# One transformer layer on one core: parts of 8, 6, 8 hidden units, x updates and one weight sum by adding transfers, interleaved down units, modulation sums dealt anew

## The chip, the cores and the metric

The kernel runs on one core of one Trainium2 chip. A core has a matrix engine (PE, with its weight loads listed as PEld), three elementwise engines (DVE, ACT, POOL) and a sync engine (SP) that mostly starts transfers; 16 DMA engines move the data. Each engine works through its own list of instructions in order and waits on semaphores for the others. The metric is the device time of one execution in microseconds: the median of the kernel before is 997.49 us over three runs (995.41 to 998.38). One more execution was profiled.

## The reference

One layer, sequence 512, width 1024, 16 heads of 64, hidden width 2816, all in float32:

```
mod = silu(c) @ w_mod + b_mod                # nine vectors of 1024: shift, scale, gate for each of three sub-layers
h = rms_norm(x, g_ffn1) * (1 + sc1) + sh1
x = x + 0.5 * (1 + ga1) * ((silu(h @ w1_gate) * (h @ w1_up)) @ w1_down)
h = rms_norm(x, g_mix) * (1 + sc2) + sh2
x = x + (1 + ga2) * mixer(h)                 # stick-breaking heads and forgetting heads, one projection in, one out
h = rms_norm(x, g_ffn2) * (1 + sc3) + sh3
x = x + 0.5 * (1 + ga3) * ((silu(h @ w2_gate) * (h @ w2_up)) @ w2_down)
```

The change touches the two feed-forward sub-layers (FFN1 and FFN2), the nine modulation vectors, and the first matmuls of the mixer.

## The kernel before, in words

**Layout and precision.** Activations lie transposed: x is eight tiles of 128 features by 512 positions. A product of two float32 matrices is made of three matmuls: each operand is split into a rounded "hi" and the rest "lo", and hi·hi, hi·lo and lo·hi are added up in PSUM (`mm3`, L129 to L132). `prep` (L122) makes a weight ready: SP starts the transfer into a `raw` tile, ACT casts it to `hi` (L125), DVE subtracts to get `lo` (L126). `raw`, `hi` and `lo` have four buffers each, so weights run ahead of their use by up to four tiles.

**A feed-forward sub-layer** (`ffn`) goes through 2816 = 22 x 128 hidden units in three parts, `FPARTS = (8, 8, 6)`. For each hidden unit of a part it makes gate and up, then `gated` (L406): ACT's silu, a DVE product `av`, ACT's cast `ah` (L414), DVE's rest `al` (L415). Then `down` multiplies the part's units by their rows of the down weight, for each of eight chunks e of 128 output features: 3 x 8 matmuls of 512 columns for a part of 8, 3 x 6 for a part of 6, into a PSUM bank of the tag `pt`, of which there are two. DVE then adds the scaled bank to x[e] (`update`, L574). So x is updated three times in each sub-layer.

**Pairs.** Units from number 8 on (FFN1) or 4 on (FFN2) are made two at a time by `block_pair` (L442): gate and up of both are a 2x2 block product done with 7 instead of 8 products, each 24 matmuls of 256 columns. It loads four weight blocks r11, r12, r21, r22 and makes s1 = r21+r22, s2 = s1-r11, s3 = r11-r21, s4 = r12-s2 by one DVE operation each (L459), each product's operand again cast by ACT (L453) and reduced to `lo` by DVE (L454). The products run in the order r11, s2, s1, r12, s3, s4, r22 and collect in three banks, `o`, `mm` and `z`.

**Modulation sums.** 56 of the 72 pieces of the modulation vectors are computed in the midst of FFN1, by `mod_next(n)`: SP loads a 512 KB tile `wm` and DVE does a multiply-and-sum (L216). `wm` has four buffers, which the DVE combinations s1 to s4 share. `mod_next` is called with 2 after units 4 to 7, with 1 after each pair, with 2 after each chunk e of a down, until none are left.

**The turn.** At the end of FFN1 and of the mixer, `turn` (L642) does the last three chunks (e5 to e7) in two halves of the sequence, H0 and H1, 256 columns each. While H1 of e5 to e7 runs, the mean square of H0 is taken (a matmul at L659, placed ahead of step 5 of e5's H1), then the inverse root, then the normalised `h` for H0 by DVE, ACT and DVE again. The first matmuls of the next stage, the V projection of the mixer (L724), begin as soon as h of H0 is there. They run for two groups of four banks; each bank is copied out when its eight k are done.

**Order.** PE's order is the order of the code. On the other engines a scheduler decides, by its own estimates; each engine's list is then fixed.

Of the kernel before, what the change touches and what calls it, by code (L numbers as in the profile page):

```python
# [8 lines left out]
F32 = mybir.dt.float32  # L9
# [6 lines left out]
P = 128  # L16
# [1 line left out]
D = 1024  # L18
KD = D // P
NF = 22  # L20
FPARTS = (8, 8, 6)
SPLIT1 = tuple(range(8, NF, 2))
SPLIT2 = tuple(range(4, NF, 2))
NPAIR = 4
# [11 lines left out]
def hybrid_layer(  # L36
# [74 lines left out]
    def bank(tag):  # L111
        return psum.tile([P, S], F32, tag=tag, name=nm(tag), bufs=PB[tag])
# [327 lines left out]
        return out  # L440

    def block_pair(w, n_w, j, T, tmp):  # L442
        raws = []
        for n in range(4):
            raw = wpool.tile([P, 2 * S], F32, tag="raw", name=nm("raw"), bufs=4)
            nc.sync.dma_start(raw, w[n_w + n])
            raws.append(raw)
        r11, r12, r21, r22 = raws

        def parts(src):  # L450
            hi = wpool.tile([P, 2 * S], F32R, tag="hi", name=nm("hi"), bufs=4)
            lo = wpool.tile([P, 2 * S], F32R, tag="lo", name=nm("lo"), bufs=4)
            nc.scalar.copy(hi, src)  # L453
            nc.vector.tensor_tensor(lo, src, hi.bitcast(F32), op=ALU.subtract)  # L454
            return hi, lo

        def combined(x0, x1, op):
            t = block_tile(tmp)
            nc.vector.tensor_tensor(t, x0, x1, op=op)  # L459
            return t  # L460

        def whole_h(k0, sl):
            return [(h["h"][k0 + k][:, sl], h["l"][k0 + k][:, sl]) for k in range(KD // 2)]

        def summed_h(n):
            sl = slice(n * 256, (n + 1) * 256)
            return [(hi[:, sl], lo[:, sl]) for hi, lo in T]

        def product(b, wt, rhs, first, last):
            for u, sl in enumerate((H0, H1)):  # L470
                for k, (rh, rl) in enumerate(rhs):
                    lh, ll = wk(wt, 4 * u + k)
                    f, e = first and u == 0 and k == 0, last and k == KD // 2 - 1
                    nc.tensor.matmul(b[:, sl], lh, rh, start=f, stop=False, skip_group_check=True)  # L474
                    nc.tensor.matmul(b[:, sl], lh, rl, start=False, stop=False, skip_group_check=True)  # L475
                    nc.tensor.matmul(b[:, sl], ll, rh, start=False, stop=e, skip_group_check=True)  # L476

        def result(x0, x1, out=None):
            if out is None:
                out = tmp.tile([P, S], F32, tag="bres", name=nm("bres"), bufs=4)  # L480
            nc.vector.tensor_tensor(out, x0, x1, op=ALU.add)
            return out

        bx, by, bz = bank("o"), bank("mm"), bank("z")
        product(bx, parts(r11), whole_h(0, H0), True, True)
        p1 = tmp.tile([P, S], F32, tag="bres", name=nm("bres"), bufs=4)
        nc.scalar.copy(p1, bx)
        s1 = combined(r21, r22, ALU.add)
        s2 = combined(s1, r11, ALU.subtract)
        product(by, parts(s2), summed_h(1), True, True)  # L490
        q = result(by, p1)
        product(bz, parts(s1), summed_h(0), True, True)
        r = result(bz, p1)
        product(bx, parts(r12), whole_h(4, H0), False, True)
        s3 = combined(r11, r21, ALU.subtract)
        product(by, parts(s3), summed_h(2), False, True)
        c22 = result(by, r, r)
        s4 = combined(r12, s2, ALU.subtract)
        product(bz, parts(s4), whole_h(4, H1), False, True)
        c12 = result(bz, q, q)  # L500
        product(by, parts(r22), summed_h(3), False, True)
        c21 = result(by, p1, p1)
        return [
            gated(j, [(H0, bx[:, H0], bx[:, H1]), (H1, c12[:, H0], c12[:, H1])], tmp),
            gated(j + 1, [(H1, c22[:, H0], c22[:, H1]), (H0, c21[:, H0], c21[:, H1])], tmp),
        ]

    def ffn(first, w, wd, gm, startup, boundary, tmp, finish=None, split=()):
        pend = list(kb) if startup else []
        blocks = {}  # L510
        n_w = 0
        f0 = 0
        for part, nf in enumerate(FPARTS):
            last_part = part == len(FPARTS) - 1
            a = []
            halves_first = first and part == 0
            units = {}
            j = -1
            while j + 1 < nf:
                j += 1  # L520
                f = f0 + j
                if f in split:
                    if "T" not in blocks:
                        blocks["T"] = block_sums(tmp)
                    a += block_pair(w, n_w, j, blocks["T"], tmp)
                    n_w += 4
                    j += 1
                    if startup:
                        mod_next(1)
                    continue  # L530
                ps = []
                for u in range(2):
                    if pend:
                        ps.append(pend.pop(0))
                        continue
                    if halves_first and j < 2:
                        if j == 0 and u == 0:
                            ws, bs = [], []
                            for i in range(4):
                                ws.append(prep(w[n_w], D, nc.gpsimd if i == 3 else None))  # L540
                                n_w += 1
                                bs.append(bank("mm" if i % 2 == 0 else "z"))
                            late = [(i, k) for i in range(4) for k in range(KD // 2, KD)]
                            for sl in (H0, H1):
                                early = [(i, k) for k in range(KD // 2) for i in range(4)]
                                for i, k in early + (late if sl is H1 else sorted(late, key=lambda s: s[1])):
                                    lh, ll = wk(ws[i], k)
                                    mm3(bs[i][:, sl], lh, ll, h["h"][k][:, sl], h["l"][k][:, sl], k == 0, k == KD - 1)
                                    if sl is H0 and (i, k) == (3, 0):
                                        finish()  # L550
                            in_order.__exit__(None, None, None)
                            units = dict(enumerate(bs))
                        ps.append(units[2 * j + u])
                        continue
                    wt = prep(w[n_w], D)
                    n_w += 1
                    b = bank("z" if u else "mm")
                    for k in range(KD):
                        lh, ll = wk(wt, k)
                        mm3(b, lh, ll, h["h"][k], h["l"][k], k == 0, k == KD - 1)  # L560
                    ps.append(b)
                a.append(gated(j, [(FULL, ps[0], ps[1])], tmp))
                if startup and f > 3:
                    mod_next(2 if part == 0 else 3)
            if startup and part == 0:
                blocks["T"] = block_sums(tmp)
            if last_part and boundary != "end":
                in_order.__enter__()
            done = down(wd, a, f0, nf, gm, boundary if last_part else None, tmp)
            f0 += nf  # L570
        return done

    def update(e, ps, gm, sl):
        nc.vector.scalar_tensor_tensor(  # L574
            out=x[e][:, sl], in0=ps[:, sl], scalar=g_col(gm)[:, e : e + 1], in1=x[e][:, sl], op0=ALU.mult, op1=ALU.add
        )

    def down(wd, a, f0, nf, gm, boundary, tmp):
        nfull = KD if boundary is None else KD - 1 if boundary == "end" else KD - NB
# [9 lines left out]
        def chunk(e):  # L589
            return wd[e, :, f0 * P : (f0 + nf) * P]  # L590

        for e in range(nfull):
            wt = prep(chunk(e), nf * P)
            ps = bank("pt")
            for step in steps(wt, ps, FULL):
                step()
            update(e, ps, gm, FULL)
            mod_next(2)
            if acc:
                acc.add(e)  # L600
            if boundary == "end":
                nc.scalar.dma_start(out[e], x[e])
# [141 lines left out]

    chunks = [v_weights(2), v_weights(3)]
    for sp in range(2):
        grp = [(ch, s, bank("mm" if s % 2 == 0 else "z")) for ch in chunks for s in (2 * sp, 2 * sp + 1)]
        for k in range(KD):
            for ch, s, b in grp:
                v_step(ch, s, k, b)  # L750
            if sp == 0 and k == 0:
                finish()
        for ch, s, b in grp:
            v_out(ch[0], s, b)
# [483 lines left out]
```

## Time and profile before

| | |
|---|---|
| median of 3 runs | 997.49 us |
| profiled execution | 999.74 us, of which the span 998.0 us |
| granted TensorE clock, mean over the span | 0.993 |
| PE busy | 976.3 us (98%), 6284 matmuls |
| DVE busy | 773.7 us (78%) |
| ACT busy | 439.0 us (44%) |
| POOL busy | 119.0 us (12%) |
| moved by DMA | 129.04 MB, mean 129 GB/s |

PE is busy nearly always, but "busy" is taken from modelled ends of matmuls that overlap, and a matmul that runs at half the clock counts as busy for twice as long. What a stage costs is read from the starts of its first and last matmul. A matmul of 512 columns that follows another without waiting starts 0.227 us after it (192 of them in the 43.52 us from 104.72 to 148.24), one of 256 columns 0.120 us after it. The stages of FFN1 lie as follows, in microseconds of the span: down of the first part 104.72 to 148.24, three pairs, the fourth, down of the second part 228.96 to 273.55, three pairs, down of the third part from 334.02, its halved chunks until 374.37, then the V projection. FFN2 ends the program; its last down begins at 961.13.

### The profile page before, as it was taken

Reading aid. Unit: us, or ns where it says so; the run is one execution under the profiler, and the core shown is the slowest. Engines: PE = TensorE matmul, PEld = TensorE weight load, DVE = VectorE, ACT = ScalarE, POOL = GpSimd, SP = SyncE. Lnnn points to the kernel's source line nnn. Section 1 sums busy time; section 2 is a strip of 40 time slices with the busy share of each in tenths; the row PEclk is TensorE's granted clock in tenths of the full one; section 3 lists DMA queues with packets and bytes.
Section 4 is the critical chain, followed back from the end, with each engine's and each line's share of the span. In section 5 each row is a group of like instructions: output and inputs, shape, how many; then the busy total and the mean of one; then the engine's idle time right before and its main releaser. Section 6 shows DMA issues by size and latency. Waiting matters only on the chain.

```text
span 998.0 us, 15752 instructions
## 1 busy us (share of the span) xinstructions
PE 976.3 (98%) x6284; PEld 869.4 (87%) x6284; DVE 773.7 (78%) x1147; ACT 439.0 (44%) x686; POOL 119.0 (12%) x131
## 2 busy tenths in 40 slices
PE   8999999999999898999999999999999999999998
PEld 7888889998899798877887877998988999889997
DVE  7999967999879966688857687698855699556962
ACT  6344224443244425587556462364432444324430
POOL 1000000000000043065413335210000000000000
PEclk9999999999999899999999999999999999999999
DMA  9985933359634832411212111214252133521231
GB/s 358 316 277 154 343 135 106 121 159 309 235 104 122 260 107 65 127 55 53 64 54 73 44 43 65 85 37 133 76 147 93 55 116 103 150 85 64 96 117 63
DMA packets 37369, 129.04 MB, mean 129 GB/s; under 512 B 4400, under 2 KB 4656, under 8 KB 37296
## 3 DMA queue, kind: packets, MB, share of 16 engines
q1 hardware_dynamic: 35712, 125.88, 38.1%
q10 hardware_dynamic: 1584, 2.16, 0.6%
q8 instruction: 49, 0.80, 0.3%
q14 instruction: 24, 0.20, 0.1%
HBM read 125.92 MB, written 2.10 MB: 128 GB/s over the span
## 4 chain that ended last, share of the span: by engine, by line
PE 76%; DVE 14%; ACT 4%; DMA 3%; issue 2%; POOL 1%; SPq 0%; ACTq 0%; DVEq 0%; POOLq 0%
PE pt L131 8%; PE pt L132 8%; PE pt L130 8%; PE mm L130 5%; PE mm L132 4%; PE mm L131 4%; PE mm L476 3%; PE mm L475 3%; PE mm L474 3%; PE o L476 3%; PE o L475 3%; PE o L474 2%; PE z L476 2%; PE z L475 2%; PE z L474 2%; DVE lo L454 2%
## 5 line engine op out<-in xcount | busy, mean ns | idle before, releaser
L125 ACT CAST hi<-raw 128x1024 fp32r<-128x1024 f32 (+2 forms) x90 | 91.5, 1021 | 142.3 <-PE pt L131 61.3
L131 PE MATMUL pt<-al,hi 128*128 128x512 f32 (+1 forms) x334 | 131.1, 392 | 2.5 <-DVE al L415 2.5
L130 PE MATMUL pt<-ah,hi 128*128 128x512 f32 (+1 forms) x334 | 130.4, 391 | 0.6 <-ACT ah L414 0.6
L132 PE MATMUL pt<-ah,lo 128*128 128x512 f32 (+1 forms) x334 | 130.4, 390 | 0.0
L126 DVE TENSOR_TENSOR lo<-raw,hi 128x1024 fp32r<-128x1024 f32 (+2 forms) x89 | 108.0, 1216 | 28.8 <-ACT hi L125 28.3
L453 ACT CAST hi<-bsum 128x1024 fp32r<-128x1024 f32 x64 | 66.8, 1051 | 113.5 <-DVE bsum L459 61.3
L474 PE MATMUL mm<-th,hi 128*128 128x256 f32 x384 | 108.7, 283 | 0.0
L475 PE MATMUL mm<-tl,hi 128*128 128x256 f32 x384 | 108.7, 283 | 0.0
L476 PE MATMUL mm<-th,lo 128*128 128x256 f32 x384 | 108.7, 283 | 0.0
L574 DVE SCALAR_TENSOR_TENSOR x<-pt,gcol,x 128x512 f32<-128x512 f32 (+1 forms) x51 | 36.3, 712 | 67.2 <-PE pt L132 67.2
L454 DVE TENSOR_TENSOR lo<-bsum,hi 128x1024 fp32r<-128x1024 f32 x64 | 78.2, 1222 | 10.8 <-ACT hi L453 10.3
L453 ACT CAST hi<-raw 128x1024 fp32r<-128x1024 f32 x48 | 50.4, 1050 | 67.5 <-PE pt L131 30.5
L130 PE MATMUL mm<-hh,hi 128*128 128x512 f32 (+1 forms) x208 | 79.6, 383 | 0.0
L132 PE MATMUL mm<-hh,lo 128*128 128x512 f32 (+1 forms) x208 | 77.9, 374 | 0.6 <-DVE lo L126 0.6
L131 PEld LDWEIGHTS pt<-al,hi 128*128 128x128 f32 x334 | 63.4, 190 | 16.8 <-DVE al L415 4.0
L131 PE MATMUL mm<-hl,hi 128*128 128x512 f32 (+1 forms) x208 | 77.8, 374 | 0.2 <-DVE hl L170 0.2
L130 PEld LDWEIGHTS pt<-ah,hi 128*128 128x128 f32 x334 | 63.3, 190 | 14.4 <-ACT ah L414 1.4
L132 PEld LDWEIGHTS pt<-ah,lo 128*128 128x128 f32 x334 | 63.4, 190 | 12.9
L474 PEld LDWEIGHTS mm<-th,hi 128*128 128x128 f32 x384 | 73.7, 192 | 0.0
L475 PEld LDWEIGHTS mm<-tl,hi 128*128 128x128 f32 x384 | 73.7, 192 | 0.0
L476 PEld LDWEIGHTS mm<-th,lo 128*128 128x128 f32 x384 | 73.7, 192 | 0.0
L476 PE MATMUL o<-hh,lo 128*128 128x256 f32 x256 | 72.4, 283 | 0.0
(349 smaller groups left out, 2565.6 us busy)
## 6 DMA issues: line engine op xcount, KB each, us to landing
raw<-w SPq DMA_DIRECT2D x80, 512.0 KB, 3.6
wm<-wmod SPq DMA_DIRECT2D x72, 512.0 KB, 5.2
raw<-w1d SPq DMA_DIRECT2D x16, 512.0 KB, 6.3
raw<-wqk SPq DMA_DIRECT2D x16, 512.0 KB, 3.5
raw<-w2d SPq DMA_DIRECT2D x16, 512.0 KB, 4.2
raw<-w1s SPq DMA_DIRECT2D x8, 512.0 KB, 5.3
raw<-wo SPq DMA_DIRECT2D x8, 512.0 KB, 3.5
raw<-w1d SPq DMA_DIRECT2D x8, 384.0 KB, 5.9
```

The costliest lines, as they stand in the source:

```text
L125: nc.scalar.copy(hi, raw)
L126: (lo_engine or nc.vector).tensor_tensor(lo, raw, hi.bitcast(F32), op=ALU.subtract)
L130: nc.tensor.matmul(ps, lh, rh, start=first, stop=False)
L131: nc.tensor.matmul(ps, lh, rl, start=False, stop=False)
L132: nc.tensor.matmul(ps, ll, rh, start=False, stop=last)
L453: nc.scalar.copy(hi, src)
L454: nc.vector.tensor_tensor(lo, src, hi.bitcast(F32), op=ALU.subtract)
L474: nc.tensor.matmul(b[:, sl], lh, rh, start=f, stop=False, skip_group_check=True)
L475: nc.tensor.matmul(b[:, sl], lh, rl, start=False, stop=False, skip_group_check=True)
L476: nc.tensor.matmul(b[:, sl], ll, rh, start=False, stop=e, skip_group_check=True)
L574: nc.vector.scalar_tensor_tensor(out=x[e][:, sl], in0=ps[:, sl], scalar=g_col(gm)[:, e : e + 1], in1=x[e][:, sl], op0=ALU.mult, op1=ALU.add)
```

## The change

Five things change:

1. `FPARTS` is (8, 6, 8) in both sub-layers: the second part has three pairs and the third four (FFN1).
2. In the first two parts of each sub-layer, x is no longer updated by DVE. ACT reads the bank and writes the scaled result to an SBUF tile (`add_far`, tag `bres`, four buffers), and a transfer started by POOL adds that tile to x[e]. 32 of the 51 updates move. The updates of the last part stay on DVE.
3. In `block_pair`, s1 = r21+r22 is made by transfers: SP loads r21 into the tile, and a transfer started by POOL adds r22 to it. r22 is also loaded by itself, so a pair has five transfers of 512 KB. s3 becomes r22-s2. The products run in the order r11, s1, s2, r12, s3, s4, r22.
4. In each down, the steps of e0 and e1 are interleaved: all but the last two units of e0, all but the last two units of e1, the last two of e0, the last two of e1.
5. `mod_next` is called with 4 after units 4 to 7, with 2 after a pair (1 for the pairs at 14 and 16 and 18, none at 20), and 2 after each e as before: the 56 sums end ahead of the third part's down. In the V projection, the second group uses the banks pt, mm, pt, o in place of mm, z, mm, z.

The halved chunks of the third part now have 8 steps of 3 matmuls in place of 6, and its five whole chunks 8 in place of 6.

```diff
-FPARTS = (8, 8, 6)
+FPARTS = (8, 6, 8)
...
     def block_pair(w, n_w, j, T, tmp):
-        raws = []
-        for n in range(4):
+        d11, d12, d21, d22 = (w[n_w + n] for n in range(4))
+
+        def load(src):
             raw = wpool.tile([P, 2 * S], F32, tag="raw", name=nm("raw"), bufs=4)
-            nc.sync.dma_start(raw, w[n_w + n])
-            raws.append(raw)
-        r11, r12, r21, r22 = raws
+            nc.sync.dma_start(raw, src)
+            return raw
+
+        s1 = load(d21)
+        nc.gpsimd.dma_start(s1, d22, accum_op=ALU.add)
+        r11, r12, r22 = load(d11), load(d12), load(d22)
...
-        s1 = combined(r21, r22, ALU.add)
+        product(bz, parts(s1), summed_h(0), True, True)
+        r = result(bz, p1)
         s2 = combined(s1, r11, ALU.subtract)
         product(by, parts(s2), summed_h(1), True, True)
         q = result(by, p1)
-        product(bz, parts(s1), summed_h(0), True, True)
-        r = result(bz, p1)
         product(bx, parts(r12), whole_h(4, H0), False, True)
-        s3 = combined(r11, r21, ALU.subtract)
+        s3 = combined(r22, s2, ALU.subtract)
...
-                        mod_next(1)
+                        mod_next(2 if f < 14 else 1 if f < NF - 2 else 0)
...
-                    mod_next(2 if part == 0 else 3)
+                    mod_next(4)
...
+    def add_far(e, ps, gm, tmp):
+        t = tmp.tile([P, S], F32, tag="bres", name=nm("step"), bufs=4)
+        nc.scalar.activation(t, ps, AF.Identity, scale=g_col(gm)[:, e : e + 1])
+        nc.gpsimd.dma_start(x[e], t, accum_op=ALU.add)
+
     def down(wd, a, f0, nf, gm, boundary, tmp):
...
-        for e in range(nfull):
+        ahead = {}
+        for e in range(2):
             wt = prep(chunk(e), nf * P)
             ps = bank("pt")
-            for step in steps(wt, ps, FULL):
+            ahead[e] = (ps, steps(wt, ps, FULL))
+            for step in ahead[e][1][: nf - 2]:
                 step()
-            update(e, ps, gm, FULL)
+        for e in range(nfull):
+            if e in ahead:
+                ps, left = ahead[e][0], ahead[e][1][nf - 2 :]
+            else:
+                wt = prep(chunk(e), nf * P)
+                ps = bank("pt")
+                left = steps(wt, ps, FULL)
+            for step in left:
+                step()
+            if boundary is None:
+                add_far(e, ps, gm, tmp)
+            else:
+                update(e, ps, gm, FULL)
             mod_next(2)
...
-        grp = [(ch, s, bank("mm" if s % 2 == 0 else "z")) for ch in chunks for s in (2 * sp, 2 * sp + 1)]
+        tags = iter(("pt", "mm", "pt", "o") if sp else ("mm", "z", "mm", "z"))
+        grp = [(ch, s, bank(next(tags))) for ch in chunks for s in (2 * sp, 2 * sp + 1)]
```

How this stands on three engines, in FFN1. Names carry the number of the instruction; `raw`, `hi` and `lo` are a weight and its two halves, `av`, `ah`, `al` a hidden unit and its two halves, `bw` the weights of the halved chunks, `wm` a modulation tile, `junk` the throw-away output of a modulation sum.

ACT, in the down of the first part, before:

```order
L414 CAST ah_847<-av_844 128x512
L125 CAST hi_1068<-raw_1067 128x1024
L105 ACTIVATE sg_921<-mm_865 128x512
L125 CAST hi_1108<-raw_1107 128x1024
L414 CAST ah_925<-av_922 128x512
L125 CAST hi_1149<-raw_1148 128x1024
L125 CAST hi_1189<-raw_1188 128x1024
L125 CAST hi_1229<-raw_1228 128x1024
L125 CAST hi_1269<-raw_1268 128x1024
```

and after the change:

```order
L414 CAST ah_951<-av_948 128x512
L437 CAST th_1016<-bsum_1009 128x1024
L125 CAST hi_1191<-raw_1190 128x1024
L583 ACTIVATE step_1076<-pt_1026,gcol 128x512
L125 CAST hi_1233<-raw_1232 128x1024
L583 ACTIVATE step_1093<-pt_1051,gcol 128x512
L125 CAST hi_1275<-raw_1274 128x1024
L583 ACTIVATE step_1135<-pt_1110,gcol 128x512
L583 ACTIVATE step_1177<-pt_1152,gcol 128x512
L125 CAST hi_1317<-raw_1316 128x1024
L583 ACTIVATE step_1221<-pt_1196,gcol 128x512
L583 ACTIVATE step_1263<-pt_1238,gcol 128x512
```

Between the casts now stand the activations that empty the banks, in the order e0, e1, e2 and so on. The one of e0 (`step_1076`) has the cast of e4's weight (`hi_1191`) ahead of it, that of e2 (`step_1135`) the cast of e6's.

DVE, from the end of the last pair into the third part's down, before:

```order
L126 TENSOR_TENSOR lo_3409<-raw_3407,hi_3408 128x768
L216 SCALAR_TENSOR_TENSOR junk_3435,mods<-wm_3433,c_bc 128x1024
L411 TENSOR_TENSOR av_3346<-sg_3345,bres_3194 128x256
L481 TENSOR_TENSOR bres_3160<-mm_3130,bres_3160 128x512
L216 SCALAR_TENSOR_TENSOR junk_3439,mods<-wm_3437,c_bc 128x1024
L415 TENSOR_TENSOR al_3352<-av_3346,ah_3351 128x512
L411 TENSOR_TENSOR av_3356<-sg_3355,bres_3160 128x256
L126 TENSOR_TENSOR lo_3447<-raw_3445,hi_3446 128x768
L216 SCALAR_TENSOR_TENSOR junk_3473,mods<-wm_3471,c_bc 128x1024
L415 TENSOR_TENSOR al_3362<-av_3356,ah_3361 128x512
L216 SCALAR_TENSOR_TENSOR junk_3477,mods<-wm_3475,c_bc 128x1024
L574 SCALAR_TENSOR_TENSOR x_80<-pt_3375,gcol,x_80 128x512
```

and after:

```order
L411 TENSOR_TENSOR av_3367<-sg_3366,bres_3245 128x256
L485 TENSOR_TENSOR bres_3183<-mm_3153,bres_3183 128x512
L415 TENSOR_TENSOR al_3373<-av_3367,ah_3372 128x512
L126 TENSOR_TENSOR lo_3494<-raw_3492,hi_3493 128x1024
L411 TENSOR_TENSOR av_3377<-sg_3376,bres_3183 128x256
L126 TENSOR_TENSOR bw_3566<-raw_3564,bw_3565 128x1024
L415 TENSOR_TENSOR al_3383<-av_3377,ah_3382 128x512
L126 TENSOR_TENSOR bw_3572<-raw_3570,bw_3571 128x1024
L126 TENSOR_TENSOR bw_3578<-raw_3576,bw_3577 128x1024
L577 SCALAR_TENSOR_TENSOR x_80<-pt_3392,gcol,x_80 128x512
L126 TENSOR_TENSOR lo_3530<-raw_3528,hi_3529 128x1024
L577 SCALAR_TENSOR_TENSOR x_81<-pt_3417,gcol,x_81 128x512
```

The modulation sums are gone from among the last two units' operations. In their place the subtractions for the halved chunks (`bw`) stand there, two of them between the last `al` and the update of x[0].

SP, at the start of the third part's down weights, before:

```order
L124 DMA raw_3369<-w1d 128x768
L124 DMA raw_3407<-w1d 128x768
L209 DMA wm_3365<-wmod 128x1024
L209 DMA wm_3395<-wmod 128x1024
L209 DMA wm_3401<-wmod 128x1024
L209 DMA wm_3433<-wmod 128x1024
L209 DMA wm_3437<-wmod 128x1024
L124 DMA raw_3445<-w1d 128x768
```

and after:

```order
L447 DMA raw_3150<-w 128x1024
L124 DMA raw_3386<-w1d 128x1024
L124 DMA raw_3411<-w1d 128x1024
L124 DMA raw_3456<-w1d 128x1024
L124 DMA raw_3492<-w1d 128x1024
L124 DMA raw_3528<-w1d 128x1024
L124 DMA raw_3564<-w1d 128x1024
L124 DMA raw_3570<-w1d 128x1024
```

The five modulation loads between the second and the third down weight are gone.

## The prediction

> **What bounds the kernel now.** I read first the page's busy times and the chain of waits that ended last, then the matmul engine's waits by releaser.
>
> ```profile
> PE 976.3 (98%) x6284; PEld 869.4 (87%) x6284; DVE 773.7 (78%) x1147; ACT 439.0 (44%) x686; POOL 119.0 (12%) x131
> PE 76%; DVE 14%; ACT 4%; DMA 3%; issue 2%; POOL 1%; SPq 0%; ACTq 0%; DVEq 0%; POOLq 0%
> PE mm L724 <- ACT hh L167: 2.8, 1, 2.8
> PE pt L131 <- DVE al L415: 2.5, 3, 1.1
> PE z L724 <- ACT V L713: 0.9, 1, 0.9
> PE pt L130 <- ACT ah L414: 0.6, 1, 0.6
> ```
>
> PE is the bound, with only 22 us (998.0 - 976.3) not busy. So taking work off DVE is worth nothing by itself; the change can win only where PE waits, or runs slowly after waiting. The four waits that it touches add up to 6.8 us, but what a wait costs is read from stages (start, length and PE's busy time; then clock, DMA share, GB/s):
>
> ```profile
> 104.72:148.24 43.52, 43.52 (x193) 1.00 0.63 233
> 228.96:273.55 44.59, 44.00 (x194) 1.00 0.76 274
> 334.02:360.58 26.56, 23.99 (x92) 0.87 0.63 211
> 374.37:381.86 7.49, 4.64 (x21) 0.77 0.48 142
> 961.13:990.03 28.90, 28.90 (x129) 1.00 0.23 82
> ```
>
> The first row is the first down of FFN1 and runs without loss: 192 matmuls of 512 columns, 43.52/192 = 0.2267 us each. The second is the same work and takes 1.07 us more. The third is FFN1's last down, 90 such matmuls, which should take 20.40 us and take 26.56: 6.16 lost. The fourth is the start of the V projection, the fifth the last down of FFN2 (126 matmuls, 28.57; 0.33 lost).
>
> **The last down of FFN1.** PE by time, the first steps of e0 and the slow stretch after them:
>
> ```profile
> 336.77 0.39 PE L130 MATMUL pt<-ah,hi 128*128 128x512 f32 x1
> 338.01 0.50 PE L131 MATMUL pt<-al,hi 128*128 128x512 f32 x1 [0.85 <-DVE al L415]
> 338.34 0.40 PE L132 MATMUL pt<-ah,lo 128*128 128x512 f32 x1
> 339.38 0.50 PE L130 MATMUL pt<-ah,hi 128*128 128x512 f32 x1 [0.64 <-ACT ah L414]
> 340.96 0.79 PE L131 MATMUL pt<-al,hi 128*128 128x512 f32 x1 [1.08 <-DVE al L415]
> 341.55 0.63 PE L132 MATMUL pt<-ah,lo 128*128 128x512 f32 x1
> 341.98 0.63 PE L130 MATMUL pt<-ah,hi 128*128 128x512 f32 x1
> 346.67 0.46 PE L132 MATMUL pt<-ah,lo 128*128 128x512 f32 x1
> ```
>
> e0 reaches units 4 and 5 at 336.8, 2.7 us after its start, before ah and al exist. It waits three times, and then 12 matmuls run 0.43 us apart (341.55 to 346.67): half rate, 2.4 us. The Trainium skill, "TensorE: Matmul & The Clock Gate", Part 1, says that an idle stretch halves the matmul clock until some 3.4 us of work have passed. By that rule the slow stretch goes with the waits; the trace agrees, with the granted clock of 0.87 in this stage.
>
> What made ah and al late, on ACT, DVE and SP:
>
> ```profile
> 317.78 9.59 SPq L209 DMA_DIRECT2D wm<-wmod  x5
> 327.41 0.42 SPq L124 DMA_DIRECT2D raw<-w1d  x1
> 333.99 0.83 ACT L125 CAST hi<-raw 128x768 fp32r<-128x768 f32 x1 [3.58 <-DMA raw<-w1d]
> 336.12 1.22 DVE L216 SCALAR_TENSOR_TENSOR junk<-wm,c_bc 128x1024 f32<-128x1024 f32 x1
> 336.68 1.28 ACT L98 ACT_TABLE_LOAD   x1
> 338.72 0.61 ACT L414 CAST ah<-av 128x512 fp32r<-128x512 f32 x1
> 339.07 1.22 DVE L216 SCALAR_TENSOR_TENSOR junk<-wm,c_bc 128x1024 f32<-128x1024 f32 x1
> 340.22 0.69 DVE L415 TENSOR_TENSOR al<-av,ah 128x512 fp32r<-128x512 f32 x1
> ```
>
> Five modulation loads sit on SP ahead of the third down weight, since their buffers wait for DVE's sums; the weight is issued at 327.41, and ACT stands 3.58 us before its cast with the silu of the last units queued behind. DVE then puts a sum of 1.22 us ahead of each al. The change takes both away (no sum and no such load after the third part's second pair), and it moves the need: with eight units interleaved, units 6 and 7 are first needed after 6+6 steps of 3 x 0.2267, 8.16 us after the start. I replay the new order with the durations above: the cast of the last down weight, silu, one cast for the halved chunks, the table load, ah at 4.3, al at 5.0 us. Margin 3 us: the whole **6.16 us** goes.
>
> The second part's down has the same shape. There I take **1.07**: units 4 and 5 of six are needed 8 steps in, at 5.44 us, against al at about 3.6 by the same replay. FFN2's last down: **0.33**.
>
> **The turn into V.**
>
> ```profile
> 369.28 0.60 PE L659 MATMUL o<-hold,ones_ms 128*128 128x256 f32 x2
> 377.38 0.48 PE L724 MATMUL mm<-hi,hh 128*128 128x256 f32 x1 [2.85 <-ACT hh L167]
> 393.05 0.39 PE L724 MATMUL z<-hi,hh 128*128 128x256 f32 x1 [0.92 <-ACT V L713]
> ```
>
> From the mean of H0 (369.28) to the end of the last halved chunk lie 1+6+6 steps of 3 x 0.12 = 4.7 us, and h came 3 us too late; then V's first matmuls ran at clock 0.77. The stage took 7.49 us for 19 matmuls of 256 columns, 2.28: 5.2 lost. With 8 steps a chunk there lie 3+8+8 steps, 6.84 us, so 2.16 us more cover. DVE's subtractions for V's weights also stood before the h operations, and they too now lie earlier against the turn's end. I take **4.9** of the 5.2, by a replay of the DVE and ACT queues in which h of H0 comes 1.3 us before its need. Bounds: 2.16 (only the cover) and 5.2.
>
> The wait at 393.05 was the second group of V for bank z, which ACT still copied out: 1.08 us late and some 0.4 of slow matmuls. With pt, mm, pt, o, free since the turn, it goes. I take **1.2**, of 0 to 1.5.
>
> **What the change adds.** Halving two steps more of each of three chunks costs 36 matmuls of 0.12 for 18 of 0.2267 in FFN1, +0.24, and a third of that in FFN2, **0.32** in all.
>
> The updates moved to ACT:
>
> ```profile
> 99.30 1.05 ACT L125 CAST hi<-raw 128x1024 fp32r<-128x1024 f32 x1 [2.92 <-issue]
> 100.26 0.58 ACT L105 ACTIVATE sg<-mm 128x512 f32<-128x512 f32 x1
> L574 DVE SCALAR_TENSOR_TENSOR x<-pt,gcol,x 128x512 f32<-128x512 f32 (+1 forms) x51 | 36.3, 712 | 67.2 <-PE pt L132 67.2
> 110.18 1.05 ACT L125 CAST hi<-raw 128x1024 fp32r<-128x1024 f32 x1 [2.44 <-PE pt L131]
> ```
>
> An activation from PSUM takes 0.58 us, DVE's update 0.71. There are two pt banks. Uninterleaved, a bank had a whole chunk (5.44 us) to be emptied; now e0's last two units are followed by e1's last two, 1.36 us, and then e2 wants e0's bank. On ACT the cast of e4 stands ahead of e0's activation, and it waits for the same event (at 110.18 it started when PE left e0): 0.96 + 0.58 + some 0.1 of signalling, 1.66 against 1.36. So 0.3 us in each of the two parts of 8, and 0.1 in each part of 6, whose cast is shorter: **0.8**. In the third part DVE updates x[0] behind two subtractions whose weights load late: by the replay between 0 and 1.5 us late, **0.3**.
>
> The trace has no adding transfer. The nearest rows (issue to landing, median us):
>
> ```profile
> raw<-w SPq DMA_DIRECT2D x80, 512.0 KB, 3.6
> raw<-w1d SPq DMA_DIRECT2D x16, 512.0 KB, 6.3
> out_dram<-x ACTq DMA_DIRECT2D x7, 256.0 KB, 2.0
> x<-x_in SPq DMA_DIRECT2D x8, 256.0 KB, 4.5
> ```
>
> An x add (256 KB) lies between 2.0 and, if it must move the tile twice under load, 9; nothing waits for it but its own `bres` tile, four chunks or 16 us later. The s1 add (512 KB) lies between 3.6 and twice 6.3, 12.6. It follows a load that starts a pair ahead, and DVE's s2 wants it about 15 us after that load lands (a pair is 7 x 24 x 0.12 = 20.2 us). Both ends fit: **0**. The Trainium skill, "DMA: Bandwidth & Descriptors", Anatomy of one DMA, gives 2.0 us plus the bytes at 436 GB/s for transfers from POOL, an estimate of 3.2 us for 512 KB; no run here shows it, and the sum would be the same.
>
> The DVE time freed (32 updates of 0.71, 16 combinations of 1.22, 42 us) I cost at nothing: no pair waits for DVE before, so it only adds slack.
>
> **Sum.** 6.16 + 1.07 + 0.33 + 4.9 + 1.2 = 13.7 gained, 0.32 + 0.8 + 0.3 = 1.4 paid: 12.2. Against the profiled 999.74 that makes 987.5. The median of the runs shown lies 2.25 below the profiled one, so I forecast 985.3.
>
> **Rivals.**
>
> *The transfers become the bound in FFN1's downs.* From 228.96 to 273.55 the engines moved 274 GB/s at a share of 0.76, so full is about 360. A chunk of the new second part lasts 4.08 us and wants 0.39 MB of weight, two modulation tiles of 0.52 and an x add of 0.26: 418 GB/s. Beyond 360 that is 0.66 us for each of eight chunks, 5 us, and 11 if an add counts double. Four buffered weights cover some of it. SP's loads would come late, ACT's casts wait, and with them the activations that now stand behind them; PE then waits for its banks. The Trainium skill says in the same page, "Issuing engines are not separate DMA queues", that transfers share the 16 engines whichever engine starts them; the trace cannot show it for POOL. Time: 5 to 8 of the gain lost, 991.5. Against it: modulation tiles aren't urgent.
>
> *The turn stays bound by its chain.* If h of H0 needs the last chunk's operations on DVE rather than the mean, more steps cover only 2.16, and the second half's mean may wait in turn. Gain 9.4: 988.
>
> *Adding transfers are slow.* From about 15 us on, each s1 add delays its pair: at 18 us, 3 us for each of 14 pairs that have no down ahead of them, less what the faster rest gains: 997.5 + 42 - 12 = 1027. At 16.2 the sides balance. For it: it is a read, a second read and a write, and started by an engine that had no transfers before. Against it: the rate of 360 would have to fall to below a tenth.
>
> *The change does less than it says:* the new ACT order (cast before activation, and the casts wait for transfers) eats each gain, 997.
>
> **How the numbers follow.** Forecast 0.58, transfers 0.15, turn 0.12, little change 0.07, slow adds 0.08. A measurement tells about 0.3% (3 us) from no change. Faster by more (below 994.5): 0.58 + 0.12 + most of 0.15, 0.83. Same: 0.09. Slower: 0.08. The range runs from 982.5 (all bounds at their better end: 2.4 less paid or more gained) to 992 (the transfers rival's middle).
>
> **What would show it.** In the changed profile FFN1's last down should start each matmul 0.227 apart with no wait for al; the windows of its downs should fit 43.8, 32.8 and 27.5 us; V should follow the last halved chunk with less than 0.5 us idle at a clock of 1.0; the banks pt should be waited for by ACT's activation for about 0.3 us once a part. Adding transfers should land within 3 to 9 us. I'd be wrong if PE's waits name pt and an activation many times in a down (transfers), or `lo` and `bsum` in each pair (slow adds), or if V's first matmul still waits for hh by over 1 us (the turn).

## The result, and the profile after

The change makes the kernel slower: 1013.5 us median of four runs (1012.98 to 1015.55) against 997.93 for the kernel before (995.41 to 999.12); ratio 1.0163, 95% interval 1.0139 to 1.0188. The forecast was 985.3.

The page of the kernel after: engines, chain of waits, queues of the DMA engines, and the issues of adding transfers (size, median us from issue to landing).

```profile
span 1011.4 us, 15971 instructions
PE 978.3 (97%) x6308; PEld 871.1 (86%) x6308; DVE 731.7 (72%) x1099; ACT 460.5 (46%) x718; POOL 158.4 (16%) x179
q1 hardware_dynamic: 35712, 125.88, 37.7%
q0 software_dynamic: 6912, 16.78, 9.2%
PE 76%; DVE 9%; DMA 5%; issue 4%; ACT 4%; POOL 1%; SPq 0%; ACTq 0%; POOLq 0%; DVEq 0%
x<-step POOLq DMA_DIRECT2D x32, 256.0 KB, 7.2
raw<-w POOLq DMA_DIRECT2D x16, 512.0 KB, 7.2
```

PE does as much as before (978.3 against 976.3 us), DVE 42 us less, as intended, and the span is 13.4 us longer. The new queue q0 is that of the adding transfers: 16.78 MB in 9.2% of 1011.4 us, 93 us, so 180 GB/s while one is worked on. The plain ones in q1 run at 125.88 MB in 381 us, 330 GB/s. Per byte an adding transfer holds the DMA engines nearly twice as long.

The stages of the kernel after, as the windows view gives them (start and end, length, PE busy and matmuls, granted clock, DMA share, GB/s): first down, the end of the first pair, second down, third down, start of V, FFN2's first two downs, one FFN2 pair.

```profile
104.44:154.50 50.06, 45.96 (x193) 0.97 0.91 284
163.13:176.25 13.12, 7.76 (x50) 0.87 0.55 149
222.51:263.63 41.12, 34.91 (x146) 0.92 0.94 278
344.63:371.86 27.23, 27.23 (x122) 1.00 0.31 98
389.97:392.63 2.66, 2.66 (x21) 1.00 0.06 20
743.04:787.09 44.05, 43.87 (x195) 1.00 0.66 158
847.56:880.52 32.96, 32.96 (x147) 1.00 0.67 159
889.14:903.42 14.28, 12.27 (x99) 1.00 0.47 126
```

The third down and the start of V run without loss, as forecast. The loss lies elsewhere. At 0.2267 and 0.120 us a matmul, the first down should take 43.52 and loses 6.5 us; the two products of the pair (5.76) lose 7.4; the second down (144 matmuls, 32.65) loses 8.5; FFN2 loses 0.5, 0.3 and, in four products (11.52), 2.8. Together 26.0. In the first two downs the DMA engines are 0.91 and 0.94 busy while they move 284 and 278 GB/s; before, they were 0.63 busy at 233 in the first and 0.76 at 274 in the second.

What PE waited for, and the longest of these waits on PE, ACT, POOL and SP, in the second down of FFN1 (start, length, instruction, idle time before it and what ended it):

```profile
PE pt L130 <- ACT step L583: 10.5, 5, 6.2
PE mm L478 <- DVE bres L485: 5.4, 3, 4.1
...
257.76 0.80 PE L130 MATMUL pt<-ah,hi 128*128 128x512 f32 x1 [6.21 <-ACT step L583]
...
251.07 1.05 ACT L457 CAST hi<-raw 128x1024 fp32r<-128x1024 f32 x1 [6.91 <-DMA raw<-w]
256.07 1.04 ACT L457 CAST hi<-raw 128x1024 fp32r<-128x1024 f32 x1 [3.95 <-DMA raw<-w]
257.02 0.68 ACT L583 ACTIVATE step<-pt,gcol 128x512 f32<-128x512 f32 x1
...
250.50 0.87 POOL L451 DMA_DIRECT2D raw<-w  x1 [8.76 <-DMA raw<-w]
...
230.16 10.40 SPq L209 DMA_DIRECT2D wm<-wmod  x6
240.61 18.12 SPq L447 DMA_DIRECT2D raw<-w  x6
```

Read from the bottom. SP spends 10.4 us on six modulation loads, since their buffers come free only as DVE's sums are done, and issues the first load of the next pair, r21 into the tile of s1, at 240.61. POOL can add r22 only once that has landed, and starts at 250.50. ACT's cast of s1 waits for the sum until 256.07. Behind that cast in ACT's queue stands the activation that empties the bank of the down (257.02), and PE, which wants the bank, stands from 251.55 on for 6.2 us and then runs at half rate (matmuls 0.43 us apart) until 260.9.

The plain loads are late as well. The six pair loads that SP issues in this down took 9.2 us in the median from issue to landing, against 5.9 in the second down of the kernel before; r11 was one of them, and ACT could not cast it before 251.07. In the first down plain loads are enough: ACT's cast at 140.29 waited for a down weight that was issued at 132.13 and landed at 140.19, and two activations that empty banks (from 141.24) stood behind it.

The pair at 163 shows something like it on DVE:

```profile
165.90 1.23 DVE L216 SCALAR_TENSOR_TENSOR junk<-wm,c_bc 128x1024 f32<-128x1024 f32 x1 [1.20 <-DMA wm<-wmod]
167.05 1.22 DVE L463 TENSOR_TENSOR bsum<-raw,raw 128x1024 f32<-128x1024 f32 x1
168.19 1.22 DVE L458 TENSOR_TENSOR lo<-bsum,hi 128x1024 fp32r<-128x1024 f32 x1
169.32 0.68 DVE L485 TENSOR_TENSOR bres<-z,bres 128x512 f32<-128x512 f32 x1
171.06 0.68 DVE L485 TENSOR_TENSOR bres<-mm,bres 128x512 f32<-128x512 f32 x1
...
171.79 0.38 PE L478 MATMUL mm<-th,hi 128*128 128x256 f32 x1 [4.15 <-DVE bres L485]
...
157.48 0.86 POOL L451 DMA_DIRECT2D raw<-w  x1 [1.22 <-DMA raw<-w]
158.02 1.21 POOL L584 DMA_DIRECT2D x<-step  x1
```

DVE's `bsum` at 167.05 is s2 of the next pair. It needs that pair's s1, whose adding transfer was started at 157.48 and landed at 166.85. Behind it stand this pair's two results, which release the banks that PE wants. But ahead of it stands a modulation sum whose own tile landed only at 165.80, and which ended at 167.05, 0.2 us after s1 was there. In this pair the late modulation tile holds the results up as much as s1 does.

### The profile page after: what moved, and what is told of

The parts are those of the page before. It is cut to its first block, busy times and chain, and to the rows that moved or that the text cites. A ratio compares the mean times of both kernels' runs of the same rounds, so it can differ in the third digit from the quotient of the medians.

```text
span 1011.4 us, 15971 instructions
## 1 busy us (share of the span) xinstructions
PE 978.3 (97%) x6308; PEld 871.1 (86%) x6308; DVE 731.7 (72%) x1099; ACT 460.5 (46%) x718; POOL 158.4 (16%) x179
## 3 DMA queue, kind: packets, MB, share of 16 engines
q1 hardware_dynamic: 35712, 125.88, 37.7%
q0 software_dynamic: 6912, 16.78, 9.2%
## 4 chain that ended last, share of the span: by engine, by line
PE 76%; DVE 9%; DMA 5%; issue 4%; ACT 4%; POOL 1%; SPq 0%; ACTq 0%; POOLq 0%; DVEq 0%
PE pt L130 6%; PE pt L131 6%; PE pt L132 6%; PE mm L130 4%; PE mm L478 4%; PE mm L480 4%; PE mm L479 4%; PE mm L132 4%; PE mm L131 4%; DMA raw<-w 4%; PE o L480 3%; PE z L478 3%; PE z L479 3%; PE z L480 3%; PE o L479 3%
## 5 line engine op out<-in xcount | busy, mean ns | idle before, releaser
L131 PE MATMUL pt<-al,hi 128*128 128x512 f32 (+1 forms) x328 | 128.1, 390 | 0.0
L132 PE MATMUL pt<-ah,lo 128*128 128x512 f32 (+1 forms) x328 | 127.8, 390 | 0.0
L457 ACT CAST hi<-raw 128x1024 fp32r<-128x1024 f32 x64 | 67.1, 1049 | 122.1 <-PE mm L479 50.8
L458 DVE TENSOR_TENSOR lo<-raw,hi 128x1024 fp32r<-128x1024 f32 x64 | 77.9, 1220 | 16.2 <-ACT hi L457 16.2
L130 PEld LDWEIGHTS pt<-ah,hi 128*128 128x128 f32 x328 | 62.4, 190 | 25.9 <-ACT step L583 13.4
L216 DVE SCALAR_TENSOR_TENSOR junk<-wm,c_bc 128x1024 f32<-128x1024 f32 x56 | 68.4, 1222 | 22.3 <-DMA wm<-wmod 21.9
L584 POOL DMA_DIRECT2D x<-step x32 | 30.5, 983 | 328.8 <-ACT step L583 204.8
```

Of the source, the lines that this page charges most:

```text
L130: nc.tensor.matmul(ps, lh, rh, start=first, stop=False)
L131: nc.tensor.matmul(ps, lh, rl, start=False, stop=False)
L132: nc.tensor.matmul(ps, ll, rh, start=False, stop=last)
L216: nc.vector.scalar_tensor_tensor(out=junk, in0=wm, scalar=1.0, in1=c_bc, op0=ALU.mult, op1=ALU.mult, accum_out=mods[:, i : i + 1])
L584: nc.gpsimd.dma_start(x[e], t, accum_op=ALU.add)
```

## The experiments

Four families of theory. **A**: s1 is late, because it is two transfers one after the other, and the instructions that wait for it hold up bank-emptying work queued behind them. **B**: the x updates on ACT are the cause, standing behind casts that wait for weights. **C**: the new dealing crowds the first two downs with modulation loads. **D**: the adding transfers occupy the DMA engines for longer than their bytes, and so make everything else late.

The runs came in three groups, each with the kernel before beside it: 996.08 us in the first, 997.21 in the second, 996.76 in the third.

### s1 by DVE

```diff
-        s1 = load(d21)
-        nc.gpsimd.dma_start(s1, d22, accum_op=ALU.add)
-        r11, r12, r22 = load(d11), load(d12), load(d22)
+        r11, r12, r21, r22 = load(d11), load(d12), load(d21), load(d22)
...
+        s1 = combined(r21, r22, ALU.add)
```

> The changed kernel with s1 = r21+r22 made by DVE again from two plain loads (four loads a pair); everything else, also the new order of the products and the x updates by ACT and adding transfers, as in the change. Theory A (the s1 tile is late, because it is a load and then an adding transfer, and casts and sums that wait for it stand ahead of bank-emptying work on ACT and DVE): the stalls of 7.4 us in FFN1's first pair, about 7 of the 8.5 us in FFN1's second down, and 2.8 us in an FFN2 pair go: 1013.5 - 17 = about 996. Theory B (the x updates on ACT are the cause, s1 is harmless): PE's waits for the activations stay, no less than 1008. Theory C (the modulation loads crowd the transfers of FFN1's first two downs): about 1010.

Measured: 1000.79 us, 1.0059 times the kernel before (1.0038 to 1.0080); 12.7 less than the change. Theory A came nearest in size, but pairs still stalled (3.8 us in FFN1's first pair, 5.1 in the pair behind the second down), with no s1 transfer left. So A isn't the whole of it: x adds alone make stalls too. In the first pair DVE is late there because it waits for modulation tiles (idle 2.75 us before 158.17 and 1.41 before 160.82).

### x by DVE

```diff
-            if boundary is None:
-                add_far(e, ps, gm, tmp)
-            else:
-                update(e, ps, gm, FULL)
+            update(e, ps, gm, FULL)
```

> The changed kernel with all x updates on DVE again; the s1 adding transfer stays. Theory B: the 6.5 us in FFN1's first down, the 8.5 us in the second and 0.8 us in FFN2's downs go: 1013.5 - 16 = about 998. Theory A: the pair stalls (7.4 and 2.8 us) stay or only shrink, and the second down is still late by a few us, since DVE's update then stands behind sums that wait for s1: about 1002. Both theories agree that it is slower than the run without any adding transfer.

Measured: 1005.22 us, ratio 1.0089 (1.0060 to 1.0118); 8.3 less than the change. Neither number was met: B expected twice the gain, and A about 3 us more. PE's waits are now for DVE's results of pairs:

```profile
PE mm L478 <- DVE bres L485: 5.1, 7, 2.0
PE o L480 <- DVE lo L458: 4.4, 1, 4.4
```

In the pair behind the second down A's mechanism stands by itself:

```profile
254.15 0.86 POOL L451 DMA_DIRECT2D raw<-w  x1 [18.52 <-DVE bsum L463]
259.84 1.22 DVE L463 TENSOR_TENSOR bsum<-raw,raw 128x1024 f32<-128x1024 f32 x1 [2.50 <-issue]
263.85 0.68 DVE L485 TENSOR_TENSOR bres<-mm,bres 128x512 f32<-128x512 f32 x1
264.59 0.39 PE L478 MATMUL mm<-th,hi 128*128 128x256 f32 x1 [1.99 <-DVE bres L485]
```

The adding transfer that POOL starts at 254.15 lands at 259.76. DVE stands idle for 2.50 us and makes the next pair's s2 at 259.84 (the row names no releaser, but the landing falls just before it). The result that releases PE's bank comes behind that, at 263.85.

### Neither

Both edits together.

> The changed kernel with neither adding transfer: s1 by DVE from plain loads and all x updates on DVE. The other parts (8, 6, 8 units, interleaved down units, dealing, banks of V, product order) stay. If the terms of the gain in the prediction hold and only the adding transfers and the work that waits for them cost time (A, B and D alike), it takes 997.5 - 12.9 = about 985. Theory C expects 6 to 10 us more, 991 to 995, since the dealing is still in it.

Measured: 989.18 us, ratio 0.9925 (0.9905 to 0.9944). The rest of the change is a gain, and the two adding transfers, with the activations on ACT that come with one of them, cost 24 us. C on its own can't be the loss: the dealing is still in this kernel, and it is faster than the kernel before. Windows of this kernel, first, second and third down and V's first group:

```profile
104.47:149.90 45.43, 43.82 (x193) 1.00 0.83 287
210.37:243.38 33.01, 32.99 (x147) 1.00 0.84 293
324.01:351.24 27.23, 27.23 (x123) 1.00 0.32 98
369.35:382.67 13.32, 12.67 (x102) 1.00 0.03 12
```

The downs move more per second than in the change (287 and 293 against 284 and 278) with engines less busy.

### x by ACT and POOL, without a transfer

```diff
-        nc.gpsimd.dma_start(x[e], t, accum_op=ALU.add)
+        nc.gpsimd.tensor_tensor(x[e], x[e], t, op=ALU.add)
```

> The changed kernel with the x add as a POOL instruction (x plus the tile that ACT wrote) in place of the adding transfer; ACT's activations keep their places, the s1 adding transfer stays. Theory D (the adding transfers' time on the DMA engines makes weights late): a third to a half of the 6.5 us in the first down and some of the pair stalls go, 1004 to 1008. Theory B in its pure form (only the activation's place behind waiting casts counts): within 3 us of the change, 1011 to 1014.

Measured: 1007.56 us, ratio 1.0114 (1.0088 to 1.0140). This is inside D's range and outside B's, though the first pair's stall grew instead of shrinking (from 7.4 to 9.5 us). Against x by DVE, ACT's activations and POOL's additions cost 2.3 us, which the intervals of the two runs don't tell from nothing; making the additions transfers costs another 5.9 (4.9 by the ratios). The run has a cost of its own, too: beside POOL's additions DVE's operations take longer, here 2.33 and 3.04 us in place of 1.22.

```profile
152.77 1.61 POOL L584 TENSOR_TENSOR x<-x,step 128x512 f32<-128x512 f32 x1 [8.08 <-ACT step L583]
153.14 2.33 DVE L458 TENSOR_TENSOR lo<-bsum,hi 128x1024 fp32r<-128x1024 f32 x1
155.39 3.04 DVE L463 TENSOR_TENSOR bsum<-raw,bsum 128x1024 f32<-128x1024 f32 x1
```

So B's mechanism is small where x is not moved by transfers, and most of the x updates' cost comes with the transfers, whether through D or through casts that D makes late.

### Adding transfers that nobody waits for

Into the run without adding transfers, the same bytes were put as adding transfers to the output in memory:

```diff
+        for n in range(2):
+            nc.gpsimd.dma_start(out[6 + n], d22[:, n * S : (n + 1) * S], accum_op=ALU.add)
...
+            if boundary is None:
+                nc.gpsimd.dma_start(out[e % 6], x[e], accum_op=ALU.add)
```

> The run without adding transfers (989.2), with adding transfers of the same number and size that nothing waits for: after each pair's loads, 512 KB of weights are added by POOL-started transfers to the output in memory, and after each x update in the first two parts 256 KB; the output is written over at the end. So only their time on the DMA engines is in it, not the waits for them nor ACT's new order. Theory D (their engine time makes the other loads late): most of the 24 us comes back, 1003 or more. Theory A+B (the instructions that wait for them are the cost): within 4 us of the run without, 989 to 993.

Measured: 1017.46 us, ratio 1.0191 (1.0168 to 1.0214). By the letter that is D, but the run is flawed: the pairs' transfers needed no data, so the scheduler put them early, on top of the program's first loads. The first down began at 112.69 in place of 104.47, and these waits are in no other run:

```profile
PE pt L132 <- DVE lo L126: 8.0, 1, 8.0
PE mm L371 <- POOL hi L357: 3.7, 1, 3.7
```

So it was made again with the pairs' transfers bound to the pair:

```diff
         nc.scalar.copy(p1, bx)
+        for n in range(2):
+            nc.gpsimd.dma_start(out[6 + n], p1, accum_op=ALU.add)
```

> As the run with idle adding transfers, but those of a pair now start in the midst of the pair: two of 256 KB, from the copy of the pair's first product (p1) to the output in memory, where before they had no data to wait for and started at the beginning of the program. Nothing waits for them. Theory D (engine time makes the other loads late): still 10 us or more above the 989.2 of the run without, stalls in FFN1's first down and its pairs, next to none in FFN2. Theory A+B: within 4 us, 989 to 993; then the 28 us of the other run were the crowded start and first down.

Measured: 996.99 us, ratio 1.0000 (0.9985 to 1.0014), 7.8 above the run without. It stalls where the change does, only less: the first down takes 46.11 us (45.43 without these transfers), the first pair loses 2.6 (and a later one 3.5), the second down 2.3. No instruction of PE, DVE or ACT waits for these transfers, so this part is engine time alone. It lies between the bounds of the two theories: about a third of the 24 us. These transfers end in memory, not on chip, and their queue is busy for 11.9% of the span against 9.2%, so I take a third as rather too much for D alone; that is argued, not shown.

### A plain second transfer

On the run with x by DVE:

```diff
-        nc.gpsimd.dma_start(s1, d22, accum_op=ALU.add)
+        nc.gpsimd.dma_start(s1, d22)
```

> The run with x by DVE and the s1 adding transfer (1005.2), with the second transfer of s1 a plain one that writes r22 over r21 (the sum r21+r22 is left out, so that s1 is wrong): the chain load, POOL's wait, second transfer stays as it is, the adding goes. Theory A (the chain of two transfers): within 4 us of 1005. Theory D (an adding transfer occupies the DMA engines for twice as long): half or more of the 16 us goes, 997 or less.

Measured: 993.57 us, ratio 0.9972 (0.9960 to 0.9983), 11.6 less than with the addition. The queue of these transfers and their issues, with the addition and without:

```profile
q0 software_dynamic: 2304, 8.39, 4.9%
raw<-w POOLq DMA_DIRECT2D x16, 512.0 KB, 7.8
```

```profile
q0 software_dynamic: 2304, 8.39, 2.5%
raw<-w POOLq DMA_DIRECT2D x16, 512.0 KB, 4.7
```

The same 2304 packets and 8.39 MB hold the engines for 4.9% of 1003.8 us, 49 us (170 GB/s), with the addition and 2.5% of 991.2, 25 us (338 GB/s), without; and they land 3.1 us sooner. The chain of two transfers remains, and its cost falls from 16.0 to 4.4 us. So the addition is most of what s1 costs. Whether by its engine time or by its own later landing, this run doesn't separate: both change.

### The dealing, with adding transfers in place

```diff
-                        mod_next(2 if f < 14 else 1 if f < NF - 2 else 0)
+                        mod_next(1)
...
-                    mod_next(4)
+                    mod_next(2 if part == 0 else 3)
```

> The changed kernel with the modulation sums dealt as before (2, 1, 2; nine in the third part's down). Theory C (the dealing crowds the transfers of FFN1's first two downs, and that is what makes the adding transfers and casts late): 8 to 12 us faster than the change, 1002 to 1006. Theories A, B, D: within 4 us of the change, since the downs carry the same two loads a chunk and only the backlog ahead of them is smaller: 1010 to 1014.

Measured: 1006.71 us, ratio 1.0094 (1.0070 to 1.0119), 6.8 less than the change, between the theories. The first down takes 44.04 us in place of 50.06; the second still loses 6.6. So the crowd of modulation loads is a condition of the loss there, though alone it costs nothing (next runs).

### What the gain is made of

From the run without adding transfers, one of the remaining parts was undone at a time: `FPARTS = (8, 8, 6)`; no interleaving (`range(2)` to `range(0)`); the dealing of before.

> The run without adding transfers (989.2), with parts of 8, 8, 6 units as before. By the prediction's term for the turn, the cover of 2.16 us and the clock behind it go again: 4 to 5 us more, and the second down needs its last units at the same time, the third at 5.4 instead of 8.2 us: 0 to 1 more. About 994.

> The run without adding transfers (989.2), without interleaving e0 and e1. The units of the last pair are then needed 4.1 us into the third down in place of 8.2, against ready at 5: about 1 us of wait and 1 to 2 of half-rate matmuls; in the second down, 2.7 us in, 1 to 2 us. Against it, the wait for a pt bank of 1.6 us in the first down goes. About 991. If the interleaving was what took the 6.2 us from the third down, 995.

> The run without adding transfers (989.2), with the modulation sums dealt as before: 2 after units 4 to 7, 1 after a pair, 2 after a chunk, so nine fall in the third part's down. If the dealing was what took the 6.2 us from the third down: about 994 to 995. If the interleaving covers it alone: 988 to 990, since the first down's transfers are less crowded (the 1.9 us lost there go).

Measured: 992.25 (ratio 0.9943, 0.9923 to 0.9963), 989.44 (0.9914, 0.9896 to 0.9933) and 989.25 (0.9915, 0.9893 to 0.9936), against 989.18. The parts are worth 3.1 us by the medians (1.8 by the ratios, as the kernel before was slower beside them), less than expected, and the wait at the turn is back with the old ones:

```profile
PE mm L742 <- ACT hh L167: 2.8, 1, 2.8
```

Interleaving and dealing are each worth nothing alone: either alone leaves little of the third down's 6.2 us (0.6 lost without the one, 27.81 us; 1.9 without the other, 29.06), and the first down gives the rest back.

Last, interleaving only from the second part on (`range(2 if f0 else 0)`):

> The run without adding transfers (989.2), with e0 and e1 interleaved only from the second part on. The 1.9 us that the first down lost, waiting for a pt bank that DVE empties behind modulation sums, should go, the 1.4 us that the second down lost without any interleaving should not come back: 987 to 988. If the wait for the bank comes from something else, 989.

Measured: 988.92 us, ratio 0.9921 (0.9905 to 0.9937). The first down's 1.9 us go, but the second down takes 33.97 us in place of 33.01. This and the run without adding transfers are equal within the measurement, and both beat both kernels. The banks of V were not undone by themselves.

## Why the prediction was wrong

**The step that failed is "Both ends fit: 0" for the adding transfers.** Their landing was bounded well: 7.2 us median for both sizes, inside 2.0 to 9 and 3.6 to 12.6. What failed is the claim behind it, that nothing needs them for 15 us. The s1 load does not start "a pair ahead" at the end of a down: SP has modulation loads ahead of it. In the second down load and addition took from 240.61 to 256 (9.1 us for the load, where the rows I went by had 3.6 and 6.3, and 5.5 for the addition), and ACT, idle since 244.2, waited first for r11 (until 251) and then for s1. And I asked only who needs s1, not what is queued behind the one who needs it: an activation on ACT, the results of the pair on DVE. The price was 16.0 us for s1 and 11.6 for x when each is alone, 24 together, where I had put zero for the transfers and 0.8 for ACT's order. How the 24 divide stays open: 7.8 come back when nothing waits for the transfers, and 11.6 of s1's 16.0 hang on the addition as such, by its engine time or by its later landing.

**The transfers rival named the mechanism and was given 0.15.** "5 us, and 11 if an add counts double" was for the second down, which lost 8.5; an addition does count double (170 against 338 GB/s). The text about casts that wait for transfers, with activations behind them, is what the trace shows. What I left out is that the same holds in the first down (6.5 lost), which I hadn't worked out. And I weighed against it that modulation tiles aren't urgent. That was wrong twice: their loads stand ahead of urgent loads on SP, and the sums that wait for late tiles stand on DVE ahead of a pair's results (165.90 above). The row that could have told me was there: a DMA share of 0.76 at 274 GB/s in the old second down, and 16.8 MB more to move, about half of it in this half of the program, at an unknown rate. An unknown rate with a share of 0.76 ahead of it should have been priced, not bounded away.

**The slow adds rival** had the right sign by the wrong point: it said that only beyond 15 us s1 delays a pair. At a median of 7.2 us it did. (Two figures there don't follow from their own sums and change nothing: 14 pairs and 12 us balance at 15.9 us, not 16.2, and 2.4 below 985.3 is 982.9, not 982.5.)

**ACT's order.** I costed the cast ahead of the activation at 0.3 and 0.1 us a part, 0.8 in all. In FFN2, where transfers are easy, it is 0.5 and 0.3 (the activation takes 0.68 us, not 0.58); that was near enough for two parts of four. In FFN1 the cast waits for its weight. In the POOL run, where x is not moved by transfers, the whole mechanism costs 2.3 us at most, within the noise.

**The terms of the gain mostly held.** Third down: 6.16 forecast, 6.13 gained (27.23 us for 120 matmuls; 26.56 for 90 before). FFN2's last down loses nothing. For the turn, the windows of the kernel before from the end of its halved chunks to V's second group, and of that group's first steps:

```profile
374.37:391.61 17.24, 14.39 (x102) 0.90 0.21 62
391.61:394.57 2.96, 1.98 (x14) 1.00 0.00 0
```

and of the kernel after:

```profile
389.97:403.31 13.34, 12.68 (x102) 1.00 0.01 4
403.31:404.75 1.44, 1.44 (x15) 1.00 0.60 114
```

The turn gained 3.9 (4.9 forecast: V's first matmuls run without a wait, but the second half's h is 0.7 us late once), the banks 1.5 (1.2). So the turn rival, 0.12, did not happen. The second down's 1.07 can't be seen in the change; without adding transfers that down loses 0.36.

**The sum without adding transfers.** Spans: 998.0 to 987.1, 10.9 less; my terms without the ACT cost give 13.0. The first down's bank wait is the largest missing term, 1.9 us: with the interleaving, e2 wants the first bank 1.36 us after e0, and DVE's update stands behind a modulation sum, as these rows of PE and DVE without adding transfers show; I had priced that on ACT only.

```profile
117.13 0.50 PE L130 MATMUL pt<-ah,hi 128*128 128x512 f32 x1 [1.61 <-DVE x L576]
...
115.19 1.22 DVE L216 SCALAR_TENSOR_TENSOR junk<-wm,c_bc 128x1024 f32<-128x1024 f32 x1
116.33 1.41 DVE L576 SCALAR_TENSOR_TENSOR x<-pt,gcol,x 128x512 f32<-128x512 f32 x2
```
By medians the gain is 6.9 (996.08 to 989.18). That the two differ I read as no effect of a part: the profiled run of before took 999.74, 2 to 4 above its medians, while the runs without adding transfers lie within 988.8 to 989.7. The terms were priced from an execution on the long side; I took off 2.25 for it, against 3.7 in that group of runs.

## What to carry to other kernels

An adding transfer is no free engine: it held the DMA engines twice as long per byte as a plain one here (170 against 338 GB/s), and a tile that is loaded and then added to was ready only after two landings and a wait on the issuing engine (240.61, 250.50 and 256 above). Before work is moved to transfers, read the DMA share of the stage where it lands, not the mean over the span (0.39 in the kernel before, 0.76 in the stage that lost most).

For a late input, don't ask only when its reader needs it, but what stands behind that reader in its queue: here a cast held up an activation, and the activation a PSUM bank. And where two edits cover the same wait, as interleaving and dealing did, either one is enough, and each looks worthless when undone.

## What the runs showed of the hardware

The rate of adding transfers, as above: 8.39 MB held the engines for 49 us with the addition and 25 without, with the same packets, and 512 KB landed in 7.8 against 4.7 us. Adding transfers into memory were busier still: 16.78 MB in 11.9% of 995.1 us, 118 us, 142 GB/s.

The page of the Trainium skill that the prediction cited for transfers from POOL ("DMA: Bandwidth & Descriptors", Anatomy of one DMA) gives by its fit an estimate of 3.2 us for 512 KB; the plain ones took 4.7 here beside other loads and the adding ones 7.8, so the measurement decides. Its sentence that all transfers share the same 16 engines (section "Issuing engines are not separate DMA queues") agrees with the run in which nobody waited: 7.8 us lost.
